# A ReGLU MLP on one core: the fallback path's transfers go to GpSimd's queue, and ten instead of eight warm-up products

## The chip, the cores and the metric

The kernel runs on one core of one Trainium2 chip. The metric is the device time of one execution in microseconds (us). Six runs of the kernel before gave a median of 309.07 us (308.9 to 309.74).

## The reference

x is 16x256x512 (4096 tokens of 512 features), w1 is 512x4096, w2 is 2048x512, all float32 draws from a normal distribution.

```
h = x @ w1
gate, value = np.split(h, 2, axis=-1)
h = np.maximum(gate, 0) * value
return (h @ w2).astype(np.float32)
```

## The kernel before, in words

There are two ways through the program. `fast_way` (from L100) computes the result in fp16 products with a seven-product (Strassen-like) scheme. Beside it, ScalarE sums squares of the inputs (L193), and `judge` and `count` (L501 to L516) turn them into one number, `flag`. `general_way` (from L50) computes the same result in plain float32 and overwrites the output; it stands behind `tc.If(unfit > 0)` on L45 and runs only if the flag says that the inputs do not fit fp16. With the inputs of the reference the flag is 0, so the body of the If is jumped over.

**The order of work.** In `fast_way` every engine's order is the order of the Python text (a manual schedule, L112). There are four sets of 1024 tokens; a set's first product fills 16 blocks of 128 hidden units, and its second product is mixed into the blocks of the next set. Operations that touch the change:

- **Warm-up, L448**: `idle(NWARM)` issues NWARM products of a zeroed tile (`idle`, L174 to L177: 128x128 weights, 512 columns, result thrown away). They need nothing but the zeroed tile.
- **First turn of x, L449**: `turn_pair(xo, 0, psw, "W")` transposes x's first 256 tokens on TensorE in float32 (L383, eight 128x128 products) and copies them out as fp16, one half by VectorE and one by ScalarE (L385). It waits for the first transfer of x (L419).
- **L450**: `cast_w(0, 0)` casts the first weight block to fp16 on ScalarE and VectorE (L401), after its transfer (L405).
- **L451, L452**: one more idle product (NFILL), then the second turn, `turn_pair(xo, 2, psx, "X")`.
- **L453**: `whole[0].gates((0,))`, the first real product (L255). From there on TensorE works almost without a pause.

SP's queue carries the early loads, the transposing loads and nearly all of the output (L324, L330, L338); GpSimd's queue carries the later weights and the fp16 copy of x (L359, L363, L366, L163); ScalarE's queue carries one small load and the very last output tile (L335).

**The end.** At L45 each engine reads the flag and branches. Transfers and engines count their progress in semaphores: eight for transfers that the hardware queues (SP, ScalarE) issue, eight for those of GpSimd's queue, and one per engine. Both ways past the If must leave these counts at the same values. On the jumped way, therefore, a small block raises the counts by what the general way would have raised them: for every semaphore that the general way uses, an instruction waits until its count is complete and adds the difference. In the kernel before, SP does this for the eight hardware-queue semaphores, 192 each (12 transfers of 16 counts). After the If comes the closing sequence of L649: SP waits for all semaphores, two per instruction, twelve instructions in this order: four for the semaphores of GpSimd's queue, eight for those of the hardware queues (the last for ScalarE's last output); then SP drains and all engines meet in a barrier that GpSimd gathers.

Of the kernel before, what the change touches and what calls it, by code (L numbers as in the profile page):

```python
# [16 lines left out]
P = 128  # L17
TH = 512
PERIOD = 7
NWARM = 8  # L20
NFILL = 1
NPLAIN = 3
HIGH, LOW = 512.0, 32.0
# [6 lines left out]
@with_exitstack  # L30
def kernel(ctx: ExitStack, tc: tile.TileContext, x, w1, w2, out):

    nc = tc.nc
    x2 = x.flatten_outer_dims()
    out2 = out.flatten_outer_dims()  # L40
    flagpool = ctx.enter_context(tc.tile_pool(name="flagpool", bufs=1))
    flag = flagpool.tile([1, 1], dt.int32, name="flag")
    with ExitStack() as fast:
        unfit = fast_way(fast, tc, x2, w1, w2, out2, flag)
    with tc.If(unfit > 0, label="general"):  # L45
        with ExitStack() as general:
            general_way(general, tc, x2, w1, w2, out2)


def general_way(ctx, tc, x2, w1, w2, out2):  # L50

    nc = tc.nc
    T, D = x2.shape
    H, DO = w2.shape
    NK, NH = D // P, H // P
    wp = ctx.enter_context(tc.tile_pool(name="g_w", bufs=1))
    xp = ctx.enter_context(tc.tile_pool(name="g_x", bufs=2))
    ps = ctx.enter_context(tc.tile_pool(name="g_ps", bufs=2, space=bass.MemoryType.PSUM))
    ident = wp.tile([P, P], F32, name="g_ident")
    make_identity(nc, ident)  # L60
    w1_sb = wp.tile([P, NK, 2 * H], F32R, name="g_w1")
    w2_sb = wp.tile([P, NH, DO], F32R, name="g_w2")
    for k in range(NK):
        for j in range(0, 2 * H, 1024):
            t = xp.tile([P, 1024], F32, name="g_t", tag="g_t")
            nc.sync.dma_start(out=t, in_=w1[k * P:(k + 1) * P, j:j + 1024])
            nc.vector.tensor_copy(out=w1_sb[:, k, j:j + 1024], in_=t)
    for h in range(NH):
        t = xp.tile([P, DO], F32, name="g_t", tag="g_t")
        nc.sync.dma_start(out=t, in_=w2[h * P:(h + 1) * P, :])  # L70
        nc.vector.tensor_copy(out=w2_sb[:, h], in_=t)
    for c in range(T // TH):
        xt = xp.tile([P, NK, TH], F32R, name="g_xt", tag="g_xt")
        for b in range(TH // P):
            t = xp.tile([P, D], F32, name="g_t", tag="g_t")
            nc.sync.dma_start(out=t, in_=x2[c * TH + b * P:c * TH + (b + 1) * P, :])
            for k in range(NK):
                p = ps.tile([P, TH], F32, name="g_p", tag="g_p")
                nc.tensor.transpose(p[:, :P], t[:, k * P:(k + 1) * P], ident)
                nc.vector.tensor_copy(out=xt[:, k, b * P:(b + 1) * P], in_=p[:, :P])  # L80
        g = xp.tile([P, NH, TH], F32R, name="g_g", tag="g_g", bufs=1)
        for h in range(NH):
            gate = ps.tile([P, TH], F32, name="g_p", tag="g_p")
            value = ps.tile([P, TH], F32, name="g_q", tag="g_q")
            for p, j in ((gate, h * P), (value, H + h * P)):
                for k in range(NK):
                    nc.tensor.matmul(p, w1_sb[:, k, j:j + P], xt[:, k, :], start=k == 0, stop=k == NK - 1)
            v = xp.tile([P, TH], F32, name="g_v", tag="g_v")
            nc.vector.tensor_copy(out=v, in_=value)
            nc.vector.scalar_tensor_tensor(out=g[:, h], in0=gate, scalar=0.0, in1=v, op0=MAX, op1=MULT)  # L90
        for b in range(TH // P):
            p = ps.tile([P, TH], F32, name="g_p", tag="g_p")
            for h in range(NH):
                nc.tensor.matmul(p[:, :DO], g[:, h, b * P:(b + 1) * P], w2_sb[:, h], start=h == 0, stop=h == NH - 1)
            o = xp.tile([P, DO], F32, name="g_o", tag="g_o")
            nc.vector.tensor_copy(out=o, in_=p[:, :DO])
            nc.sync.dma_start(out=out2[c * TH + b * P:c * TH + (b + 1) * P, :], in_=o)


def fast_way(ctx, tc, x2, w1, w2, out2, flag):  # L100
# [73 lines left out]
    def idle(n):  # L174
        for _ in range(n):
            t = psy.tile([P, TH], F32, name="Y", tag="Y")
            nc.tensor.matmul(t, warm_b[:, :P], warm_b[:, :TH], start=True, stop=True)  # L177
# [201 lines left out]
    def turn_pair(o, b0, pool, nm):  # L379
        for b in (b0, b0 + 1):  # L380
            ps = pool.tile([P, 4, P], F32, name=nm, tag=nm)
            for e in range(4):
                nc.tensor.transpose(ps[:, e], xf[:, b, e * P:(e + 1) * P], ident[F32])  # L383
            copy = nc.scalar.copy if b % 2 else nc.vector.tensor_copy
            copy(out=o["A1"][:, :, b * P:(b + 1) * P], in_=ps)  # L385
# [61 lines left out]

    idle(NWARM)  # L448
    turn_pair(xo, 0, psw, "W")  # L449
# [204 lines left out]
```

## Time and profile before

| what | value |
|---|---|
| median of six runs | 309.07 us (308.9 to 309.74) |
| the profiled execution: time | 308.86 us |
| the profiled execution: span, first to last instruction | 307.1 us |
| PE busy | 300.6 us, 98% of the span |
| first and last PE product | 1.28 us, about 302.6 us |
| first real product (L255) | 8.48 us |
| DVE, ACT, POOL busy | 71%, 62%, 45% |
| transfers by the hardware queue of SP and by GpSimd's queue | 20.32 MB, 10.75 MB |

The profiled execution's own time is 1.76 us above its span; what lies in that difference the profile does not show. "PE" is TensorE's products, "PEld" its weight loads; a letter q (SPq, POOLq) means an engine's sequencer, which issues transfers and handles semaphores and branches and is not counted as busy. A row `line engine op xcount: a/b/c, s to t` gives the shortest, median and longest duration in ns, and the first and last start in us.

### The profile page before, as it was taken

To read this page: it belongs to the slowest core of one execution; us is meant where nothing else is said; L and a number is where in the kernel's file an instruction comes from. 1 tells how busy PE (TensorE), PEld (TensorE's weight loads), DVE (VectorE), ACT (ScalarE), POOL (GpSimd) and SP (SyncE) were. 2 spreads that over 40 slices of the span, in tenths; PEclk is the share of its full clock that TensorE was granted. 3 is DMA by queue.
4 is the path that set the end of the run, shared out by engine and by line. 5 is a ranking of instruction groups with operands and counts; after the bars stand their busy time and mean duration, and the time that the engine had idled before them with its cause. 6 is when DMAs were issued, how large, how long until landed. Compare 5 with 4: busy or idle time off the path is not lost.

```text
span 307.1 us, 5116 instructions
## 1 busy us (share of the span) xinstructions
PE 300.6 (98%) x1868; PEld 182.7 (59%) x1868; DVE 219.3 (71%) x346; ACT 189.7 (62%) x457; POOL 139.7 (45%) x127
## 2 busy tenths in 40 slices
PE   7999999999999999999999999999999999999994
PEld 4574444588844444478864444458884444447883
DVE  1798898896468888884347888885526888888401
ACT  2557776568576676737856767656857667673230
POOL 1749999810004438990002344994000433899000
PEclk9999999999999999999999999999999999999999
DMA  6999986989615740064130000036311101000123
GB/s 224 306 204 205 204 205 194 184 159 191 225 66 102 140 102 1 2 129 146 68 139 14 22 34 2 0 69 140 138 70 68 34 4 33 0 2 0 70 87 124
DMA packets 34410, 31.54 MB, mean 103 GB/s; under 512 B 14448, under 2 KB 28784, under 8 KB 34160
## 3 DMA queue, kind: packets, MB, share of 16 engines
q1 hardware_dynamic: 24608, 20.32, 21.7%
q0 software_dynamic: 9104, 10.75, 21.1%
q8 instruction: 15, 0.25, 0.3%
q10 hardware_dynamic: 672, 0.13, 0.2%
q14 instruction: 11, 0.09, 0.1%
HBM read 24.12 MB, written 11.53 MB: 116 GB/s over the span
## 4 chain that ended last, share of the span: by engine, by line
PE 96%; DMA 2%; ACT 0%; SPq 0%; issue 0%; ACTq 0%
PE Y L205 26%; PE X L205 17%; PE W L205 17%; PE Y L291 14%; PE X L291 9%; PE W L291 9%; DMA g<-in_w_dram 2%; PE W L255 2%; PE X L255 1%; PE Y L255 1%; SPq L419 0%; PE X L391 0%; ACT Y L212 0%; ACT wr L401 0%; ACT pv L333 0%
## 5 line engine op out<-in xcount | busy, mean ns | idle before, releaser
L280 POOL TENSOR_TENSOR g_S<-g 128x512 f16<-128x512 f16 (+1 forms) x46 | 58.1, 1292 | 126.3 <-DVE g L244 126.3
L205 PEld LDWEIGHTS <-wt 128*128 128x128 f16 x488 | 47.7, 98 | 55.8 <-issue 0.3
L205 PE MATMUL X<-x_A,wr 128*128 128x512 f16 x244 | 72.6, 379 | 0.1
L205 PE MATMUL Y<-x_S,wt 128*128 128x512 f16 x244 | 72.6, 379 | 0.0
L205 PEld LDWEIGHTS <-wr 128*128 128x128 f16 x366 | 35.8, 98 | 41.4 <-issue 0.4
L232 DVE SCALAR_TENSOR_TENSOR cc<-W,pu 128x512 f32<-128x512 f32 x61 | 42.2, 692 | 24.1 <-ACT pu L226 24.0
L212 ACT COPY Y<-X 128x512 f32<-128x512 f32 x61 | 34.8, 570 | 38.0 <-PE X L205 37.6
L291 PEld LDWEIGHTS <-g_S 128*128 128x128 f16 x512 | 50.0, 98 | 5.8
L238 DVE SCALAR_TENSOR_TENSOR cc<-Y,pu 128x512 f32<-128x512 f32 x61 | 42.2, 691 | 6.3
L226 ACT ACTIVATE pu<-Y 128x512 f32<-128x512 f32 x61 | 36.4, 596 | 13.9 <-PE Y L205 13.9
L233 DVE SCALAR_TENSOR_TENSOR g<-X,cc 128x512 f16<-128x512 f32 x61 | 42.2, 691 | 2.4
L244 DVE SCALAR_TENSOR_TENSOR g<-Y,cc 128x512 f16<-128x512 f32 x61 | 41.6, 682 | 1.8 <-PE Y L205 1.8
L291 PEld LDWEIGHTS <-g 128*128 128x128 f16 x384 | 37.6, 98 | 8.2
L219 ACT ACTIVATE pu<-W 128x512 f32<-128x512 f32 x61 | 36.8, 603 | 0.3 <-PE W L205 0.3
L205 PE MATMUL Y<-x_A,wt 128*128 128x512 f16 x122 | 36.3, 379 | 0.0
L205 PE MATMUL W<-x_S,wt 128*128 128x512 f16 x122 | 36.3, 379 | 0.0
L205 PE MATMUL W<-x_S,wr 128*128 128x512 f16 x122 | 36.3, 379 | 0.0
L291 PE MATMUL X<-w,g 128*128 128x256 f16 x256 | 31.2, 273 | 0.0
L291 PE MATMUL Y<-v,g_S 128*128 128x256 f16 x256 | 30.6, 273 | 0.0
L321 DVE SCALAR_TENSOR_TENSOR o<-W,pv 128x256 f32<-128x256 f32 x16 | 6.8, 424 | 29.7 <-PE W L291 29.7
L280 POOL TENSOR_TENSOR g_S<-g,g_S 128x512 f16<-128x512 f16 x18 | 21.7, 1208 | 1.4
L280 POOL TENSOR_TENSOR g_S<-g_S,g 128x512 f16<-128x512 f16 x18 | 20.8, 1155 | 1.4
(76 smaller groups left out, 285.7 us busy)
## 6 DMA issues: line engine op xcount, KB each, us to landing
out_dram<-o SPq DMA_DIRECT2D x14, 256.0 KB, 2.1
out_dram<-pv SPq DMA_DIRECT2D x14, 256.0 KB, 2.0
x<-in_x_dram POOLq DMA_DIRECT2D x3, 1024.0 KB, 9.1
xn<-x SPq DMA_DIRECT2D x12, 256.0 KB, 3.2
g_S<-in_x_dram SPq DMA_DIRECT2D x4, 512.0 KB, 6.5
wr<-in_w_dram POOLq DMA_DIRECT2D x4, 512.0 KB, 13.0
w<-in_w_dram POOLq DMA_DIRECT2D x4, 512.0 KB, 15.4
g<-in_w_dram SPq DMA_DIRECT2D x2, 512.0 KB, 6.5
```

Of the source, the lines that this page charges most:

```text
L205: nc.tensor.matmul(ps, W(wn, self.jb)[:, b], self.xo[xn][:, b, :], start=fresh and b == 0, stop=b == 1, skip_group_check=True)
L212: nc.scalar.copy(out=self.Y, in_=self.X)
L219: nc.scalar.activation(self.p5, self.W, COPY, scale=GS)
L226: nc.scalar.activation(self.u2, self.Y, COPY, scale=-GS)
L232: nc.vector.scalar_tensor_tensor(out=self.c12, in0=self.W, scalar=GS, in1=self.u2, op0=MULT, op1=ADD)
L233: nc.vector.scalar_tensor_tensor(out=self.g[:, self.jb, :TH], in0=self.X, scalar=0.0, in1=self.c12, op0=MAX, op1=MULT)
L238: nc.vector.scalar_tensor_tensor(out=self.c22, in0=self.Y, scalar=-GS, in1=self.p5, op0=MULT, op1=ADD)
L244: nc.vector.scalar_tensor_tensor(out=self.g[:, self.jb, TH:], in0=self.Y, scalar=0.0, in1=self.c22, op0=MAX, op1=MULT)
L255: nc.tensor.matmul(ps[:, ts], W(names[e // 2], self.jb)[:, e % 2], self.a[:, e, ts], start=e == 0, stop=e == 3, skip_group_check=True)
L280: eng.tensor_tensor(go[n][:, h0:h1], go[i0][:, h0:h1], go[i1][:, h0:h1], op=op)
L291: nc.tensor.matmul(ps, go[gn][:, k, b * P:(b + 1) * P], V[vn][:, k, :], start=fresh and k == 0, stop=k == NHC - 1, skip_group_check=True)
L321: nc.vector.scalar_tensor_tensor(out=d["o1"][:, HALF:], in0=d["W"], scalar=1 / GS, in1=d["pu"][:, 1], op0=MULT, op1=ADD)
```

## The change

The constant NWARM goes from 8 to 10, so that two more products of the zeroed tile stand in front of the first turn of x. In `general_way` all four kinds of transfer (w1, w2, x, output: 16 + 16 + 32 + 32 = 96) are issued by GpSimd instead of SP.

```diff
-NWARM = 8
+NWARM = 10
...
             t = xp.tile([P, 1024], F32, name="g_t", tag="g_t")
-            nc.sync.dma_start(out=t, in_=w1[k * P:(k + 1) * P, j:j + 1024])
+            nc.gpsimd.dma_start(out=t, in_=w1[k * P:(k + 1) * P, j:j + 1024])
...
-        nc.sync.dma_start(out=t, in_=w2[h * P:(h + 1) * P, :])
+        nc.gpsimd.dma_start(out=t, in_=w2[h * P:(h + 1) * P, :])
...
-            nc.sync.dma_start(out=t, in_=x2[c * TH + b * P:c * TH + (b + 1) * P, :])
+            nc.gpsimd.dma_start(out=t, in_=x2[c * TH + b * P:c * TH + (b + 1) * P, :])
...
-            nc.sync.dma_start(out=out2[c * TH + b * P:c * TH + (b + 1) * P, :], in_=o)
+            nc.gpsimd.dma_start(out=out2[c * TH + b * P:c * TH + (b + 1) * P, :], in_=o)
```

In the built program this changes two more things. On the jumped way, the general way now uses no hardware-queue semaphore, so SP's block of eight instructions (wait for a count, add 192) is gone; instead GpSimd's sequencer waits for the eight semaphores of its own queue and adds 192 to each with one instruction, INC_SWDGE_SEM. The closing sequence of L649 is the same twelve waits in the same order, with other counts. Up to the branch, the instructions of SP, GpSimd, VectorE and ScalarE stand as before; TensorE has the two added products with their two weight loads.

## The prediction

> **What bounds the kernel now.** I read the page's chain first, then the chain in order of time at both ends, since the change touches only the start and what lies behind the branch of L45.
>
> ```profile
> PE 96%; DMA 2%; ACT 0%; SPq 0%; issue 0%; ACTq 0%
> ...
> 1.95 6.05 DMA g<-in_w_dram
> 8.02 0.41 ACT wr L401
> 8.48 1.10 PE X L255 x8
> ...
> 302.97 0.38 ACT pv L333
> ```
>
> TensorE carries the chain from 8.48 us to about 303 us. Ahead of it stands not TensorE's warm-up but a transfer: the first weight block lands at 8.00, is cast by ScalarE (L401), and then the first real product starts. The 0.38 us of ScalarE at 302.97 ends the chain of work, yet the span runs to 307.07. The chain does not name those last 3.7 us; the sequencers do. First the timeline of the start:
>
> ```profile
> 1.28 3.59 PE L177 MATMUL Y<-warm 128*128 128x512 f16 x8 [1.28 <-DVE warm L167]
> 5.47 1.60 PE L383 MATMUL W<-ident,g_S 128*128 128x128 f32 x8 [0.60 <-DMA g_S<-in_x_dram]
> 8.02 0.40 ACT L401 CAST wr<-g 128x256 f16<-128x256 f32 x1 [0.33 <-DMA g<-in_w_dram]
> 8.02 0.29 DVE L401 CAST wr<-g 128x256 f16<-128x256 f32 x1 [0.73 <-DMA g<-in_w_dram]
> 8.33 0.58 ACT L385 CAST x_A<-X 128x512 f16<-128x512 f32 x1
> ```
>
> TensorE ends its eight warm-up products and sits idle until x has landed; ScalarE and VectorE, done with the first turn's copies, sit idle 0.33 and 0.73 us until the weights land. Then the last microseconds, from the views of L45 and L649 (the rows of L45 come from narrow windows, so that each shows one start):
>
> ```profile
> L45 SPq COMPARE_BRANCH  x1: 70/70/70, 302.9 to 302.9; - x1
> L45 SPq EVENT_SEMAPHORE  x1: 17/17/17, 303.4 to 303.4; - x1
> L45 SPq EVENT_SEMAPHORE  x4: 17/17/17, 303.5 to 303.7; - x4
> L45 SPq EVENT_SEMAPHORE  x1: 17/17/17, 304.1 to 304.1; - x1
> L45 SPq EVENT_SEMAPHORE  x1: 17/17/17, 305.1 to 305.1; - x1
> L45 SPq EVENT_SEMAPHORE  x1: 17/17/17, 305.4 to 305.4; - x1
> ...
> L649 SPq EVENT_SEMAPHORE  x12: 28/28/28, 305.5 to 306.1; - x12
> L649 SPq DRAIN  x1: 13/13/13, 306.2 to 306.2; - x1
> ```
>
> SP's first five instructions of the block follow each other within 0.1 us, but the last three come at 304.1, 305.1 and 305.4: they wait for the last three output transfers, issued at 301.67, 302.50 and 303.38, which land after 2.4, 2.6 and 2.0 us (the view of the output tensor gives "min/median/max: 2.0/2.4/2.6"). Only when the very last has landed, at 305.387, does SP begin the twelve waits of L649. By then all of them are met, and still they run one after the other: the single starts in the trace are 305.453, 305.520 and so on to 306.129, 0.061 us apart, and the drain is at 306.194. The barrier then ends the span at 307.07. So twelve idle formalities stand behind the last landing.
>
> **The change part by part: the end.** SP's eight instructions at L45 go. SP then branches at 302.885 and can begin L649's twelve at about 303.40 (the 0.52 us from branch to first instruction is as now). Four for GpSimd's semaphores and the first five of the hardware queue's are met already: 9 x 0.061 = 0.55 us, to 303.95. The next two wait for the same landings as now (304.11 and 305.11), the last for 305.39. So only one instead of twelve stands behind the last landing, and the drain comes at 305.387 + 0.065 = 305.45 instead of 306.194: 0.74 us earlier (306.194 - 305.452). After it nothing is late but the barrier, which SP enters last: ScalarE and TensorE enter it at 304.0 and 303.1, VectorE at 302.0. The barrier's 0.88 us stay.
>
> What the change puts in their place lies on GpSimd: five waits and one INC_SWDGE_SEM. Behind them on that engine stands only its own drain (292.1, 1.62 us) and the barrier; SP waits for it with its first four instructions of L649. GpSimd branches at 291.8 and is at 292.02 on the jumped way, with all its transfers landed long ago (the last was issued at 105 us). The cover is 303.40 - 292.02 = 11.4 us, and 13.4 us until the last landing. Five waits at 0.1 us are 0.5 us. The trace has INC_SWDGE_SEM once, at 0.1 us, as a reset: 27 ns. Adding to eight semaphores by software may cost more; the nearest large row is that drain, 1.62 us. Both ends (0.03 to 1.6) are far inside the cover: 0 on the path. A gain from it is excluded, since GpSimd waits in the barrier anyway.
>
> The 96 moved transfers themselves cost nothing: the profile has no row of L66, L70, L76 or L97. [...] I take 0. No other queue is passed: up to the branch, SP's and GpSimd's instructions stand as before.
>
> **The change part by part: the start.** The eight products start 0.427 us apart, the last at 4.24, so the next could start at 4.67. Two more start at 4.67 and 5.09 and free TensorE at 5.52; the first transpose started at 5.47. The two products thus lie in the 0.80 us in which TensorE waited for x, and push the turn back by 0.05 us. A push of the first turn is hidden by the 0.33 us that ScalarE waits before the cast of L401. The second turn's last result is there at 8.165 (last transpose 7.892 + 0.273), and ScalarE's copy of it starts at 8.33, behind that cast: 0.17 us of cover. Without that cover, 0.05 us would pass to the second real group. So 0 on the path. If x landed 0.2 us earlier in a run, the push would be 0.25 us, of which some 0.1 us would show.
>
> Could the products help? TensorE's clock goes up during the first turn:
>
> ```profile
> L383 PE MATMUL W<-ident,g_S x8: 272/408/447, 5.5 to 6.8; 128*128 128x128 f32 x8
> L383 PE MATMUL X<-ident,g_S x8: 272/272/273, 7.1 to 7.9; 128*128 128x128 f32 x8
> ```
>
> The trace's record of the granted clock puts the step at 6.59 us; the second turn is at full speed. [...] By the rows, the clock rose 5.3 us after the first product with the idle 0.8 us and the transposes inside, so nothing is left to save: even an earlier step only lengthens the wait for the weights. I take the rows: 0, [...] 0.1 us of loss from the push.
>
> **The sum** against the profiled execution: 308.86 - 0.74 + 0 = 308.12, span 306.33. It lies 0.21 us below the median of the runs before; the same 0.74 off the median, 309.07, is 308.33 us, 0.24% less.
>
> **The rivals.**
> 1. *The end gains, the start takes part of it.* x lands earlier or the clock steps later in most runs, and the push shows: 0.1 to 0.4 us, so 308.45 to 308.75. [...] Against: the measured cover of 0.17 and 0.33 us, and TensorE's further small waits up to 9 us.
> 2. *The change does nothing at the end*: another wait takes the place of the twelve, [...] the waits are slow for another reason: 309.07. Against: 1.5 us of cover, since SP has to wait for the last landing anyway.
> 3. *Slower: GpSimd's INC_SWDGE_SEM.* SP's first wait of L649 needs its result. Its price decides from 11.4 us on (SP late), and from 13.4 + 0.7 us on the kernel is slower than before; at 16 us it would be 16 - 13.4 = 2.6 us past the last landing, less 0.06: about 310.9. For it: the trace has no row of this form. Against: 27 ns for the reset form.
> 4. *The clock was missed in most runs and is now caught*: up to 0.2 us more in the median, 308.1.
>
> **How the numbers follow.** A measurement of this kernel tells about 0.2% (0.6 us) from no change, so "faster" begins at 308.45. The likeliest case, 308.33, gets 0.65, of which 0.05 may fall just above that line by scatter; rival 1 0.17, rival 2 0.08, rival 3 0.04, rival 4 0.06. Faster: 0.60 + 0.06 = 0.66. Same: 0.05 + 0.17 + 0.08 = 0.30. Slower: 0.04. The range takes in the likeliest case with the scatter of the runs (about 0.15), rival 4 and rival 1: 308.05 to 308.85.
>
> **What would show it.** In the changed profile: no SPq EVENT_SEMAPHORE of L45; of L649's twelve, nine before 304.0 and the last within 0.1 us of the last landing; the SP drain 2.0 us + 0.1 after ScalarE's last issue; span near 306.3. POOLq's INC_SWDGE_SEM of L45 ends before 300. At the start ten warm products ending near 5.5, the transposes following with no wait, and the first L255 product at 8.48 as before. I am wrong if L255 starts later than 8.6, or if SP's twelve waits again follow the last landing.

## The result, and the profile after

The changed kernel took 308.48 us (median of 35 runs, 308.18 to 309.0); the kernel before, run beside it, 309.18 us (72 runs, 308.8 to 311.38). The medians lie 0.70 us apart, the lowest runs 0.62. The ratio is 0.9967 with a 95% interval of 0.9958 to 0.9976. It is further from 1 than the medians (0.9977), because the kernel before has something the changed one has not: 14 of its 72 runs lie between 310.5 and 311.4 us, with none between 309.8 and 310.5; none of the 35 runs of the changed kernel lies above 309.0. The means are 309.54 and 308.52.

The two views of the end, in the changed kernel: the sequencers at L45, and SP at L649 in narrow windows.

```profile
L45 POOLq INC_SWDGE_SEM  x1: 562/562/562, 292.8 to 292.8; - x1
L45 SPq COMPARE_BRANCH  x1: 64/64/64, 302.9 to 302.9; - x1
...
L649 SPq EVENT_SEMAPHORE  x9: 28/28/28, 303.1 to 303.7; - x9
L649 SPq EVENT_SEMAPHORE  x1: 28/28/28, 304.7 to 304.7; - x1
L649 SPq EVENT_SEMAPHORE  x1: 28/28/28, 305.6 to 305.6; - x1
L649 SPq EVENT_SEMAPHORE  x1: 28/28/28, 305.9 to 305.9; - x1
L649 SPq DRAIN  x1: 13/13/13, 306.0 to 306.0; - x1
```

SP has no semaphore instruction left at L45. Nine of the twelve waits are over by 303.7, the last three come one by one with the last three landings, and the drain follows the last at once (305.908, then 305.973). GpSimd's part is done by 293.4, long before SP's first wait at 303.1.

Yet the span of this one execution fell only from 307.07 to 306.85 us, not by 0.74. The view of the output tensor says why: in it the last three outputs landed later after their issue than before.

```profile
L335 ACTq DMA_DIRECT2D out_dram<-pv x1: 377/377/377, 303.4 to 303.4; - x1
...
DMA to landing us min/median/max: 2.5/2.9/3.0
```

Before it was 2.0/2.4/2.6. ScalarE's output is issued at 303.43 and seen at 305.91, 0.52 us later than before (0.05 of it because it was issued later): 0.74 - 0.52 = 0.22. In the profiles of the ten experiments below, the same output is seen 2.0 to 2.5 us after its issue, in nine of them by 2.2 us, so this is scatter of the landing, not a cost of the change; the medians show the rest.

The start, in the timeline of the changed kernel:

```profile
1.28 4.45 PE L177 MATMUL Y<-warm 128*128 128x512 f16 x10 [1.28 <-DVE warm L167]
5.52 1.55 PE L383 MATMUL W<-ident,g_S 128*128 128x128 f32 x8
8.08 0.41 ACT L401 CAST wr<-g 128x256 f16<-128x256 f32 x1 [0.38 <-DMA g<-in_w_dram]
8.54 1.10 PE L255 MATMUL X<-x_A,wr 128*128 128x256 f16 x8 [0.37 <-ACT wr L401]
```

The wait for x in front of the turn is gone from the row of the transposes, which start 0.05 us later (5.52 for 5.47). ScalarE still waits for the weights, now 0.38 us; they land 0.06 us later than before, and so the first real product is at 8.54 for 8.48.

### The profile page after: what moved, and what is told of

Same layout as the page of the kernel before. It is cut to its first block, busy times and chain, and to the rows that moved or that the text cites. A ratio compares the mean times of both kernels' runs of the same rounds, so it can differ in the third digit from the quotient of the medians.

```text
span 306.9 us, 5117 instructions
## 1 busy us (share of the span) xinstructions
PE 301.2 (98%) x1870; PEld 182.9 (60%) x1870; DVE 219.2 (71%) x346; ACT 189.7 (62%) x457; POOL 139.7 (46%) x127
## 4 chain that ended last, share of the span: by engine, by line
PE 96%; DMA 2%; ACT 0%; SPq 0%; issue 0%; ACTq 0%
PE Y L205 26%; PE X L205 17%; PE W L205 17%; PE Y L291 14%; PE X L291 9%; PE W L291 9%; DMA g<-in_w_dram 2%; PE W L255 2%; PE X L255 1%; PE Y L255 1%; SPq L419 0%; PE X L391 0%; ACT Y L212 0%; ACT wr L401 0%; ACT pv L333 0%
```

## The experiments

**Theory.** The end gives the median its gain: the twelve waits of L649 no longer stand behind the last landing. The two products do nothing to the median, but they take away the long runs, supposedly because with the wait for x filled TensorE's clock rises in good time in every run. **Rivals**: the products shorten all runs; the queue takes away the long runs; not the place of the waits counts but the number of SP's instructions or of moved transfers.

Each experiment is compared with the kernel before, run on the same chip. "Long" means more than 1.3 us above the lowest run of the same kernel.

**One part of the change alone.** The first keeps the ten products and leaves the transfers on SP:

```diff
-            nc.gpsimd.dma_start(out=t, in_=w1[...])
+            nc.sync.dma_start(out=t, in_=w1[...])
```

and the three other transfers of the general way in the same manner.

> Ten warm-up products, general way's transfers on SP as before. Theory (the end's gain comes from the moved transfers; the products take away the runs at 310.5 to 311.4 us, 14 of the 72 runs of before, by letting the clock rise in every run): SP's eight instructions at L45 are back, the twelve waits of L649 follow the last landing, so the median stays at about 309.1 us, but no run lies above 310. Rival A (the products themselves shorten the common runs): median 308.5. Rival B (the runs at 311 belong to the queue, not to the products): median 309.1 with one run in five near 311.

Measured: 309.20 us (22 runs) against 309.27 (55 runs), ratio 0.9996 (0.9990 to 1.0003), highest run 309.79. The median gain is gone, and the twelve waits again follow the last landing (305.506):

```profile
L649 SPq EVENT_SEMAPHORE  x12: 28/28/28, 305.6 to 306.2; - x12
```

There is no long run. The second keeps the queue:

```diff
-NWARM = 10
+NWARM = 8
```

> Eight warm-up products, general way's transfers on GpSimd's queue. Theory: no SP instruction at L45, twelve waits of L649 begin at about 303.1 us, median of the common runs 0.7 us below before (about 308.4), and one run in five about 2 us longer (near 310.3). Rival A (products shorten the common runs): common runs at 309.1. Rival B (the queue takes the long runs away): no run above 309.5.

Measured: 308.64 us (22 runs) against 309.27, ratio 0.9979 (0.9969 to 0.9989): 0.63 us less. Three of the 22 runs are long (309.65, 309.75, 309.92), as are 3 of the 55 of before (310.51 to 311.04). So the queue moves the median, and it does not take away the long runs; the products do not move the median. The first two rivals fall. That the products take away the long runs is not shown by these two kernels alone: with long runs as rare as 3 in 55, none in 22 comes by chance in about one case of three. The counts over all experiments stand below.

**Where the waits stand.** Two kernels differ only in how many of the general way's first transfers (which do not run) go back to SP, five or eight:

```diff
-            nc.gpsimd.dma_start(out=t, in_=w1[...])
+            q = nc.sync if k * 4 + j // 1024 < 5 else nc.gpsimd
+            q.dma_start(out=t, in_=w1[...])
```

> As the changed kernel, but the first five transfers of the general way (w1, not run here) go back to SP. SP then has five of the eight instructions at L45, for the hardware semaphores 0 to 4, whose last transfers land early; the three for the late ones are absent. Theory (what counts is that the twelve waits of L649 do not start after the last landing): five more instructions at 0.06 to 0.1 us lie before 304 us, gain kept, about 308.5. Rival (what counts is the number of instructions on SP, eight saved): five of eight come back, so five eighths of the 0.7 us, about 308.9.

> As the changed kernel, but the first eight transfers of the general way go back to SP: all eight instructions at L45 are back, the last of them for ScalarE's last output. Theory: the twelve waits of L649 again follow the last landing, 11 x 0.061 = 0.7 us lost against the changed kernel, about 309.2, without runs above 310. Rival (number of transfers on the queue counts: 8 of 96): about 308.5, as the changed kernel.

Measured: with five, 308.58 us (10 runs), ratio 0.9973 (0.9963 to 0.9983), the whole gain; with eight, 309.17 us (14 runs), ratio 0.9992 (0.9983 to 1.0001), none of it. Five instructions cost nothing, three more cost it all. SP's views, first with five:

```profile
L45 SPq EVENT_SEMAPHORE  x5: 17/17/17, 303.0 to 303.4; - x5
...
L650 SPq EVENT_SEMAPHORE  x10: 27/28/28, 303.4 to 304.0; - x10
L650 SPq EVENT_SEMAPHORE  x1: 28/28/28, 305.2 to 305.2; - x1
L650 SPq EVENT_SEMAPHORE  x1: 28/28/28, 305.6 to 305.6; - x1
```

and with eight:

```profile
L45 SPq EVENT_SEMAPHORE  x5: 17/17/17, 303.0 to 303.4; - x5
L45 SPq EVENT_SEMAPHORE  x2: 17/17/17, 303.9 to 305.1; - x2
L45 SPq EVENT_SEMAPHORE  x1: 17/17/17, 305.4 to 305.4; - x1
...
L650 SPq EVENT_SEMAPHORE  x12: 27/28/28, 305.5 to 306.2; - x12
```

(The lines are one further down, since the edit adds one.) The last wait that needs the landing comes at 305.555 and 305.438; the drain follows at 305.622 with five and at 306.254 with eight, 0.067 and 0.816 us later. The difference, 0.75 us, is the predicted 0.74. The number of instructions and of moved transfers (91 and 88 of 96) does not decide, so the third rival falls.

**The order inside the twelve.** One more tiny load at the start turns the assignment of semaphores by one:

```diff
     nc.scalar.dma_start(out=first, in_=w1_v[:, :, 0, 0])
+    first2 = wpool.tile([P, 4], F32, name="first2")
+    nc.scalar.dma_start(out=first2, in_=w1_v[:, :, 0, 0])
```

> As the changed kernel, with one more tiny load at the start (2 KB, result unused) on ScalarE's queue. It turns the assignment of the hardware semaphores by one, so that ScalarE's last output, the last to land, counts on semaphore 0, whose wait is the fifth of L649's twelve. Theory (waits behind the one for the last landing cost 0.061 us each): seven stand behind it, 7 x 0.061 = 0.43 us more than the changed kernel, about 308.95. Rival (where the last landing stands in the row does not matter): 308.5.

Measured: 309.05 us (13 runs, no long one), ratio 0.9996 (0.9987 to 1.0004), 0.22 us below the 309.27 of before on that chip; the changed kernel is 0.70 below its own. So some 0.48 us are lost again, for the 0.43 expected. The end shows the mechanism:

```profile
L651 SPq EVENT_SEMAPHORE  x4: 27/28/28, 303.5 to 303.7; - x4
L651 SPq EVENT_SEMAPHORE  x8: 28/28/28, 305.8 to 306.2; - x8
```

SP stops at the fifth wait until the last landing, and seven met waits stand behind it. From that wait to the drain it takes 0.49 us (305.771 to 306.261), against 0.07 in the changed kernel: 0.43 us more, as expected. But the median does not measure this alone. In this execution the start came later too, which was not expected:

```profile
5.96 1.34 PE L385 MATMUL W<-ident,g_S 128*128 128x128 f32 x8 [0.23 <-DMA g_S<-in_x_dram]
8.70 0.40 ACT L403 CAST wr<-g 128x256 f16<-128x256 f32 x1 [0.78 <-DMA g<-in_w_dram]
9.15 0.61 PE L257 MATMUL X<-x_A,wr 128*128 128x256 f16 x4 [0.77 <-ACT wr L403]
```

The first real product starts at 9.15 us (8.54 in the changed kernel), and TensorE's last one 0.32 us later. It is likely that the load does this: while it is issued, SP's first two weight loads take 1.44 us to issue, against 1.02 in the changed kernel. So it is the trace, not the 0.48 us of the medians, that shows what a load of 2 KB at the start costs at the end.

**The clock.** Three warm-up products and none between the turns (one run). The two cases are that the clock rises behind work that is mostly transposes, and that it rises only behind products:

> As the changed kernel, but with three warm-up products instead of ten and none between the turns. [...] Time: 1 to 3 us above the changed kernel in both cases.

The trace's record of the granted clock has the step at 10.16 us. The one run took 309.25 us, 0.77 above the changed kernel's median and so less than the 1 to 3 expected. The products show the step:

```profile
L383 PE MATMUL W<-ident,g_S x8: 421/421/447, 5.6 to 7.1; 128*128 128x128 f32 x8
L383 PE MATMUL X<-ident,g_S x8: 421/421/421, 7.3 to 8.8; 128*128 128x128 f32 x8
...
L255 PE MATMUL X<-x_A,wr x8: 272/400/421, 9.0 to 10.4; 128*128 128x256 f16 x8
```

All 16 transposes run at half speed (0.21 us from one start to the next; 0.11 at full speed in the second turn of the kernel before), and the speed changes inside the first real group. Real products had then run for only 1.1 us, and from 5.60 us to their start at 9.04 TensorE had run nothing but transposes. In the next experiment 2.74 us of warm-up products were not enough: the eight transposes behind them still ran at half speed. So the transposes probably counted; this is inferred from two executions.

Six products instead of ten (`NWARM = 6`):

> As the changed kernel, but with six warm-up products. Theory (the products in front of the turn fill the wait for x[...]): the gap before the turn is 1.7 us, so far more runs than one in seven lie 1.3 to 2 us above the common ones: median between 309 and 310.5. Rival (the long runs have nothing to do with the warm-up): median 308.5, as the changed kernel.

Measured: 309.37 us (21 runs, 309.0 to 310.44) against 309.27, ratio 1.0003 (0.9995 to 1.0010): the 0.7 us that the end gives are lost again at the start, in most runs. All 21 lie 0.5 to 2.0 us above the changed kernel's median; so by the definition above, which starts from a kernel's own lowest run, only one of them is long.

```profile
1.28 2.74 PE L177 MATMUL Y<-warm 128*128 128x512 f16 x6 [1.28 <-DVE warm L167]
5.44 1.94 PE L383 MATMUL W<-ident,g_S 128*128 128x128 f32 x8 [1.42 <-DMA g_S<-in_x_dram]
...
9.02 0.60 PE L255 MATMUL X<-x_A,wr 128*128 128x256 f16 x4
```

With a wait of 1.42 us in front of the turn, the clock rises at 8.69 us and the first real product is at 9.02. Then the two added products in another place, between the turns of x:

```diff
-NWARM = 10
-NFILL = 1
+NWARM = 8
+NFILL = 3
```

> As the changed kernel, but the two added products stand between the two turns of x (three there, eight in front). Theory (what matters for the clock is that the wait for x is filled, not the number of products): the wait stays open, so one run in seven lies more than 1.3 us above the common ones; and the second turn comes up to 0.43 us later, of which 0.17 is covered, median 308.5 to 308.9. Rival (the number of products in the first 8 us matters): no long runs.

Measured: 308.79 us (22 runs) against 309.52 (30 runs on that chip), ratio 0.9977 (0.9965 to 0.9989), and three long runs (310.15, 310.42, 310.50). The same number of products did not take the long runs away while the wait for x stayed open. Twelve products (`NWARM = 12`):

> As the changed kernel, but with twelve warm-up products. Theory (ten just fill the wait for x; the cover behind it is 0.17 to 0.33 us): two more push the first turn by 0.43 us (clock up early) to 0.85 us (clock still at half), so the first real product comes 0.1 to 0.6 us later and the median is 0.2 to 0.5 us above the changed kernel, 308.7 to 309.0, still without runs 1.3 us above the common ones. Rival (more warm-up always helps): 308.4 or less.

Measured: 308.65 us (9 runs, 308.43 to 309.13) against the same 309.52, ratio 0.9974 (0.9962 to 0.9987). The loss that I expected did not come. In this execution the clock rose at 4.79 us, so the last products took half the time (twelve took 4.48 us, and ten 4.45 in the changed kernel):

```profile
1.28 4.48 PE L177 MATMUL Y<-warm 128*128 128x512 f16 x12 [1.28 <-DVE warm L167]
5.59 1.04 PE L383 MATMUL W<-ident,g_S 128*128 128x128 f32 x8
...
8.51 1.10 PE L255 MATMUL X<-x_A,wr 128*128 128x256 f16 x8 [0.79 <-ACT wr L401]
```

Nine runs are too few to say what twelve cost where the clock rises late.

**Counts of long runs.** Eight products in front of the first turn: 14 of 72, 3 of 55, 0 of 51 and 5 of 30 runs of before on four occasions, 3 of 22 with the queue alone, 3 of 22 with two between the turns; 28 of 252. Ten or twelve in front, without the next experiment: 0 of 103. Since the occasions differ, each is compared with itself: 0 of 35 beside 14 of 72, 0 of 46 beside 6 of 77, 0 of 13 beside 0 of 51, 0 of 9 beside 8 of 52. If the products made no difference, the first split alone would come by chance in about one case of 400. On the fourth occasion the runs of before have no gap at the limit: three more of the 30 lie 1.2 to 1.3 us above the lowest.

**The weights first.** To see whether the first real product waits for the weights, their first load is split, so that its first half comes sooner; the unused load on ScalarE's queue goes, to keep the assignment of semaphores:

```diff
-    first = wpool.tile([P, 4], F32, name="first")
-    nc.scalar.dma_start(out=first, in_=w1_v[:, :, 0, 0])
...
-    fetch_wl(0, 0, 2)
+    fetch_wl(0, 0)
+    fetch_wl(1, 0)
```

> As the changed kernel, but the first weight load (512 KB for two blocks) is split into two of 256 KB, so that the first block lands earlier; the unused 2 KB load on ScalarE's queue goes, so that the assignment of semaphores stays. Theory (the first real product waits for the weights, not for TensorE): they land some 0.6 us earlier, then the transposes' end at 8.17 is the bound: first real product near 8.2 instead of 8.5, about 0.2 to 0.3 us less, 308.2. Rival (one more issue on SP pushes all later loads by 0.5 us, and TensorE waits there): same or slower, 308.5 to 309.

Measured: 308.30 us (22 runs, 307.52 to 309.82) against 309.27, ratio 0.9974 (0.9963 to 0.9985). Theory and rival are both seen in the timeline:

```profile
8.01 0.61 PE L253 MATMUL X<-x_A,wr 128*128 128x256 f16 x4
...
10.07 0.71 ACT L399 CAST wr<-g 128x256 f16<-128x256 f32 x2 [1.03 <-DMA g<-in_w_dram]
...
10.53 1.90 PE L253 MATMUL W<-x_A,wr 128*128 128x512 f16 x8 [0.28 <-ACT wr L399]
```

The first real product comes 0.5 us sooner, and the next weights come later: ScalarE waits 1.03 us for them and TensorE then waits for ScalarE. The lowest run is the lowest of all, but the runs scatter over 2.3 us, and their mean (308.52) is that of the changed kernel. By the definition above 8 of the 22 are long, though ten products stand in front. Whether these runs come from the later weights or from the clock was not traced; that is why they stand outside the counts.

## Why the prediction was right, point by point

- **The end** was right in mechanism and size. The working gave 0.74 us; five against eight transfers on SP gives 0.75 in the traces; the queue alone gives 0.63 in the median, the whole change 0.70. The median itself, 308.48, lies 0.15 above the 308.33 forecast and so in the stretch given to rival 1; but 0.11 of the 0.15 is the kernel before, which had 309.18 here and not 309.07. Rival 1 is not what happened: the products alone leave the median as it was (0.9996), so the start took nothing. Rival 2 falls by the queue alone. For rival 4 (up to 0.2 us more) the products alone leave 0.07 us, by which their median is below that of before. The branch of SP into the closing sequence took 0.20 us and not the 0.52 of before, so the first nine waits ended at 303.70 and not at 303.95; nothing depended on it.
- **GpSimd's share** costs nothing: INC_SWDGE_SEM took 0.56 us at 292.8, inside the bounds of 0.03 to 1.6 and the cover of 11.4 us. Rival 3 falls. The moved transfers cost nothing either: none of them runs, and the queue alone is 0.63 us faster.
- **The push of the first turn** was 0.05 us as worked out, and hidden.
- **The span of the profiled execution** was forecast at 306.33 and was 306.85: the landing of the last output was taken as fixed at 2.0 us after its issue, and it scatters to 2.5.
- **The gain of the products** is the term that was mis-sized. "I take the rows: 0" holds for the median: products alone give 0.9996. But that is luck of the measure: a median does not move with a minority of long runs, and by the means the change is worth 1.01 us, not 0.74. I read the 0 from one execution, in which the clock came in time. One run in nine with eight products is long. In the 72 runs the 14 long ones have a mean of 310.91 us and the others of 309.20, which is 14 x 1.71 / 72 = 0.33 us of the mean, and with the 0.7 of the end makes the 1.01. But one execution does not show the others: in the profiles the step lies at quite different times, as the next point lists. The run of 309.74, the highest of the six of before, lies among the common ones.
- **The clock's step** stood at no fixed time. In the record of the granted clock it lay at 6.59, 6.55, 4.44, 5.33, 5.63, 5.28, 6.53, 6.47, 6.29 and 4.79 us in the ten profiles with eight to twelve products, though the products began at 1.28 us in each; with six it lay at 8.69 and with three at 10.16. What sets it no trace shows.

What is shown: with the wait for x filled, or nearly so, there is no long run among the 103 counted, and with the same number of products in another place there are three in 22. What is inferred: that they are runs in which the clock rose late. No long run was caught with a profile.

The waits for x in front of the first turn bear on it. The warm-up products start 0.43 us apart at half clock; count the wait from the time at which one more could have started. It was 0.80 us in the kernel before (4.67 to 5.47) and 0.81 with two products between the turns (4.67 to 5.48), and in both profiles the clock rose during the first turn, at 6.59 and 6.29 us. With six products it was 1.63 us, and the clock rose only at 8.69. Whether there is a length from which on the clock comes late, and where, is not shown. How late would x have to be? In the profile with one more load its turn began at 5.96 us; with eight products that would leave a wait of 1.29 us. But there the added load had probably delayed x. In the other profiles the turn began by 5.60 us, which with eight products leaves 0.93 us (estimates from these numbers), and whether that is too long no profile shows. The size fits only in part: the two executions with a late step, at 8.69 and 10.16 us, took 0.60 and 0.77 us more than the changed kernel's median, and the long runs are 1.7 us above the common ones; but with six products, where the wait for x was 1.63 us in the profile, the runs reach 2.0 above that median. Why one occasion had no long run among 51 stays open.

## What to carry to other kernels

Look at what the sequencers do after the last transfer has landed: here met waits still cost 0.06 us each when they stood behind the late one, and eight transfers in a branch that never runs put them there (0.75 us in the traces). The order of the closing sequence followed from how transfers are counted: one load more put seven met waits behind the late one, 0.43 us. And a warm-up that reached to the first turn of x without a hole, or nearly so, had no long run among 103; such a gain is seen in many runs, not in one profile.

## What was not expected of the hardware

The last three outputs landed 2.0 to 2.6 us after their issue in the profile of the kernel before, 2.5 to 3.0 in that of the changed kernel, and 2.0 to 3.1 over all twelve profiles; in the changed kernel's profile this put the last landing some 0.5 us later than before. From its branch to its first instruction behind it, SP took 0.52 us in the two kernels whose general way has all its transfers on SP, and 0.20 us in the other ten.
